# A two-layer hybrid mixer backbone on one core: reciprocals, TensorE's first waits, VectorE's share of the adaLN product, Fourier loads and the last square

## The chip, the cores and the metric

The kernel runs on one core of a Trainium2 chip. The metric is the time in microseconds (us) that the device reports for one execution; the median of several runs is given. The engines are TensorE (PE; its weight loads are listed as PEld), VectorE (DVE), ScalarE (ACT), GpSimd (POOL) and SyncE (SP). DMA transfers are issued here from the queues of SP and, where the text says so, of ACT; all of them share the core's 16 DMA engines.

## The reference

What is computed, cut to what matters:

```python
D_MODEL, SEQ, CTX_LEN, DEPTH = 2048, 256, 256, 2      # everything in float32

def rmsnorm(x, g):
    return x * lax.rsqrt(jnp.mean(x * x, axis=-1, keepdims=True) + EPS) * g

for l in range(DEPTH):
    last = l == DEPTH - 1
    shift, scale, gate = jnp.split(silu(c) @ ada_w[l] + ada_b[l], 3, axis=-1)
    shift_c, scale_c, gate_c = jnp.split(silu(c_ctx) @ ada_w[l] + ada_b[l], 3, axis=-1)
    h = rmsnorm(x, norm_g[l]) * (1.0 + scale[:, None]) + shift[:, None]
    hc = rmsnorm(xc, norm_g[l]) * (1.0 + scale_c) + shift_c
    # one projection to q, k, v, pool channels, Fourier channels and gate; k and v alone for hc in the last layer
    q, k, v, up, uf, g = split_proj(h @ w_in[l])
    ...
    att = latent_attention(rope(rmsnorm(q)), rope(rmsnorm(k)), v, kc, vc)
    mixed = concat([att, multiscale_pool(up, ...), fourier_mix(uf, fourier_w[l])])
    x = x + gate[:, None] * ((mixed * silu(g)) @ w_out[l])
    # in the first layer the same for xc, with attention to the context alone
return rmsnorm(x, final_norm_g)
```

The 256 latent and 256 context tokens stand side by side as 512 columns. The vectors c and c_ctx are the two "v" of the code.

## The kernel before

**Precision and weights.** A projection's matmul is done as three: each operand is split into a high part rounded for TensorE and a low rest. `wpiece` loads a piece of a weight matrix (raw), ACT casts it (whi) and DVE subtracts (wlo); the pool wp has three buffers of each, so the load of the fourth piece waits until DVE is done with the first. `make_h` makes the normed and modulated activations h of one 128-row block in the same two parts: DVE multiplies x by the reciprocal root (xn), scales and shifts it with the adaLN columns ab, ACT casts, DVE subtracts.

**The start (`startup`).** `stats(g)` squares four 128-row blocks of x (three squares on ACT, one on DVE), adds them in pairs on DVE, and PE multiplies each sum by a matrix of ones. That sums over partitions, for the latent half into the PSUM tile sm and for the context half into mm. `norm()` runs the last statistics, takes the roots of both halves on ACT and the reciprocal of the first; the second reciprocal stands in the loop, ahead of the second half of the first block's h.

The adaLN columns of shift and scale come in ten groups (`GROUPS`, of one or two 128-column blocks each). A group has four quarters of the 2048 input rows. `ND[j]` of them go to DVE: `dvec(j)` loads the quarter, and each scalar_tensor_tensor multiplies it by silu(c), which lies broadcast over the partitions in cq, and sums it into abq. The other quarters go to PE (`piece` loads one, `ada_part` issues four groups of 32-column matmuls with silu(c), cs, into one PSUM tile a). Then ACT copies a out (ev), PE transposes it, and DVE reduces it (red), adds the DVE quarters, the bias and the 1, and makes h. The silu(c) row that cq is broadcast from is made in `load_cb` from an input cb, stored to DRAM (cd) and read back by partition_broadcast.

There is one PSUM buffer of this kind, so the first `ada_part` of the next group waits until DVE's reduction has read the last. Between the pieces, `work(n)` issues up to n matmuls of a backlog: the products of the first input-projection chunk and of some gate columns with the h blocks that exist already. The order on PE in the start is exactly the written one (tc.manual_schedule); on the other engines a scheduler sorts by priority, which tc.high_priority changes (`DLOW`, -60, for the DVE quarters). Every DMA of the start is issued from SP's queue, and a load waits there until its buffer is free, with everything behind it; the ada quarters share four buffers (`ST`).

**After the start.** `pool_tables(0)` and `rope_tables(0)` load the tables of layer 0; `fourier_tables` loads its own (fw, the Fourier map; cct, the cosine matrices; dft) when the projection's second chunk runs, and PE forms cct times fw with them (L404). DVE meanwhile multiplies the next layer's adaLN weights (L189, ajunk<-araw,cbt). `pool_branch` has its last matmul in L347, and DVE evacuates it in L349.

**The end (`out_tok`).** The last output projection runs in four chunks of 512 columns with tokens on the partitions, two token tiles tt. `evac(a, ch, tt)` multiplies by the gate row (L758), adds the residual (L759) and squares with a running sum (L761). After chunk 3 it sums the four columns (L766), takes root and reciprocal (L767, L768), scales the four quarters on ACT and DVE (L773 to L777) and issues four stores (L778) for each tt.

Of the kernel before, what the change touches and what calls it, by code (L numbers as in the profile page):

```python
# [20 lines left out]
P = 128  # L21
# [12 lines left out]
ND = (0, 0, 0, 0, 0, 1, 1, 1, 2, 2)  # L34
# [14 lines left out]
LOW = -400  # L49
PRE = 6  # L50
# [5 lines left out]
def backbone(  # L56
# [4 lines left out]
    cb: bass.AP,  # L61
# [92 lines left out]
    def load_cb():  # L154
        crow = t2("crow", (32, P))
        nc.sync.dma_start(crow, cb)
# [217 lines left out]

    def pool_tables(l):
# [14 lines left out]
    def fourier_tables(l):  # L390
        fwt = t2("fw", (P, 512))
        nc.sync.dma_start(fwt, fw[l])
        cct = t2("cct", (P, 2, P))
        nc.sync.dma_start(cct, cc)
# [321 lines left out]
    def out_tok(xs, m, korder):  # L716
# [26 lines left out]
        side.add("turn", turn(), 2.0)  # L743
        ss = [sp.tile([P, 4], F32, tag=f"ssq{tt}", bufs=1, name=f"ssq{tt}") for tt in range(2)]
# [8 lines left out]
        def evac(a, ch, tt):  # L753
# [7 lines left out]
            S.activation(sq, x, AF.Square, accum_out=ss[tt][:, ch : ch + 1])  # L761
# [4 lines left out]
            V.tensor_reduce(r[:, 0:1], ss[tt], axis=AX.X, op=ALU.add)  # L766
            S.activation(r[:, 1:2], r[:, 0:1], AF.Sqrt, bias=epst, scale=1.0 / D)  # L767
            V.reciprocal(r[:, 1:2], r[:, 1:2])  # L768
            for q in (0, 3, 1, 2):
# [8 lines left out]
                nc.sync.dma_start(out[tt, :, cq_], o)  # L778
# [43 lines left out]
    load_cb()  # L822
# [6 lines left out]
    def startup():  # L829
        st = tc.tile_pool(name="st", bufs=ST)  # L830
        with st as st:
# [4 lines left out]
            S.activation(ctmp, cv, AF.Tanh, scale=0.5)  # L836
            V.tensor_scalar(ctmp, ctmp, 1.0, 0.5, op0=ALU.add, op1=ALU.mult)
            V.tensor_mul(cs[:, :, 0:2], ctmp.rearrange("p (k v) -> p k v", v=2), cv.rearrange("p (k v) -> p k v", v=2))
            rstd = const.tile([P, T], F32, tag="rstd", name="rstd0")
            dum = sp.tile([P, 1], F32, tag="dum", name="dum0")  # L840
            S.activation(dum, ctmp[:, 0:1], AF.Sqrt)
            ss = [smt(), mmt()]

            def stats(g):
                q = [t2("sq") for _ in range(4)]
                for j in range(4):
# [3 lines left out]
                    else:  # L850
                        S.activation(q[j], x, AF.Square)
                    if j % 2:
                        V.tensor_add(q[j - 1], q[j - 1], q[j])
                        for o, c in zip(ss, halves):
                            PE.matmul(o[:, :N], ones, q[j - 1][:, c], start=g == 0 and j == 1, stop=g == 3 and j == 3)
# [3 lines left out]
            def norm():  # L859
# [3 lines left out]
                V.reciprocal(rstd[:, halves[0]], rstd[:, halves[0]])  # L863
# [103 lines left out]

            with tc.manual_schedule(engines={mybir.EngineType.PE}):
                for g in range(3):
                    stats(g)  # L970
                for j, gs in enumerate(GROUPS):
# [4 lines left out]
                    for kk in range(npc):  # L976
                        if j == 0 and kk == 1:
                            load_x(3, 1)
                        if kk == npc - 1 and j + 1 < len(GROUPS):
# [9 lines left out]
                        ada_part(a, raws[kk], kk, kk == 0, kk == npc - 1, w_)  # L989
                        work(RATE * gs // 2)  # L990
                    ev = t2("ev")
                    S.copy(ev[:, :w_], a[:, :w_])
                    work(4)
                    for q in range(2 * gs):
                        PE.transpose(a[:, q * P : q * P + P], ev[:, q * P : q * P + P], idt)
                    work(4)
                    red = sp.tile([P, 2, gs, 2], F32, tag="red", name=name("red"))
                    V.tensor_reduce(
# [153 lines left out]
```

## Time and profile before

| | |
|---|---|
| median of 3 runs | 1078.14 us (1077.66 to 1080.66) |
| profiled execution | 1079.1 us, of which the profile's span is 1077.2 us |
| mean granted clock of TensorE | 0.992 |
| busy: PE / PEld / DVE / ACT | 97% / 78% / 79% / 45% of the span |
| moved by DMA | 234.15 MB, mean 217 GB/s |
| costliest lines on PE | L336, L337, L338 (the three matmuls of a product), 17% of the chain of waits each |

A row of the timeline gives the start and the duration in us, the engine, the line of the code, the operation, what it writes and reads, and the shape. In brackets stands the time for which the engine was idle just before, and what ended the wait. "SPq" rows are the issues of DMAs on SP's queue, where neighbours of one line are drawn together (x3). A row of the busy time by stretches gives the window, its length, the busy time of each engine with its count of instructions, and then the clock that TensorE was granted (1.00 is full), the busy share of the DMA engines and their GB/s. Times count from the span's start.

### The profile page before, as it was taken

How to read it: one execution, taken by the hardware profiler on the slowest of the kernel's cores; microseconds unless marked ns; L12 is line 12 of the kernel's file. 1: busy time of each engine (PE TensorE's matmuls, PEld its weight loads, DVE VectorE, ACT ScalarE, POOL GpSimd, SP SyncE). 2: the span in 40 equal slices, each digit the busy share in tenths (PEclk: the TensorE clock that was granted, in tenths of full speed). 3: DMA queues.
4: the chain of work that ended last, by engine and by line, in shares of the span. 5: the costliest groups of instructions: out<-in, count | busy, mean ns of one | idle time of the engine just before them, and what ended most of it. 6: DMA issues, size and time to landing. Idle time of an engine off the chain costs nothing.

```text
span 1077.2 us, 14001 instructions
## 1 busy us (share of the span) xinstructions
PE 1045.6 (97%) x5065; PEld 842.2 (78%) x5065; DVE 846.3 (79%) x1566; ACT 480.5 (45%) x807; POOL 0.2 (0%) x4
## 2 busy tenths in 40 slices
PE   5999899999999999999999999999999999999996
PEld 3466577788787888888888888888888888888885
DVE  6458656998999879997999887589656888776564
ACT  5233234323413765642532223288326768547443
POOL 0000000000000000000000000000000000000000
PEclk9999999999999999999999999999999999999998
DMA  9999857457685334457786657435765565776563
GB/s 355 414 368 345 277 200 239 157 190 233 200 266 195 96 122 155 157 195 259 251 286 218 198 195 262 139 127 190 246 229 170 159 195 184 236 262 215 180 213 115
DMA packets 64133, 234.15 MB, mean 217 GB/s; under 512 B 7153, under 2 KB 8257, under 8 KB 60353
## 3 DMA queue, kind: packets, MB, share of 16 engines
q1 hardware_dynamic: 64064, 233.28, 63.4%
q8 instruction: 39, 0.64, 0.3%
q14 instruction: 30, 0.24, 0.1%
HBM read 231.12 MB, written 2.12 MB: 217 GB/s over the span
## 4 chain that ended last, share of the span: by engine, by line
PE 66%; DVE 6%; issue 3%; ACT 1%; DMA 1%; ACTq 0%; SPq 0%; DVEq 0%
PE mm L336 17%; PE mm L338 17%; PE mm L337 17%; PE mm L312 5%; DVE ajunk L189 3%; PE mm L313 2%; PE sm L337 2%; PE sm L336 2%; PE sm L338 2%; DVE wlo L139 1%; PE sm L557 1%; DMA cbt<-cd 1%; PE sm L520 1%; DMA araw<-in_adar 0%; ACT whi L138 0%
## 5 line engine op out<-in xcount | busy, mean ns | idle before, releaser
L138 ACT CAST whi<-raw 128x1024 fp32r<-128x1024 f32 (+1 forms) x216 | 219.9, 1019 | 333.5 <-PE mm L338 108.5
L139 DVE TENSOR_TENSOR wlo<-raw,whi 128x1024 fp32r<-128x1024 f32 (+1 forms) x216 | 255.1, 1182 | 104.4 <-ACT whi L138 103.2
L189 DVE SCALAR_TENSOR_TENSOR ajunk<-araw,cbt 128x1024 bf16<-128x1024 f32 x224 | 273.6, 1221 | 48.5 <-DMA araw<-in_adar 35.2
L336 PE MATMUL mm<-whi,h 128*128 128x512 f32 x416 | 167.5, 403 | 0.0
L337 PE MATMUL mm<-wlo,h 128*128 128x512 f32 x416 | 162.8, 391 | 0.0
L338 PE MATMUL mm<-whi,h 128*128 128x512 f32 x416 | 162.8, 391 | 0.0
L336 PE MATMUL mm<-m,whi 128*128 128x512 f32 (+1 forms) x272 | 102.7, 377 | 0.0
L338 PE MATMUL mm<-m,wlo 128*128 128x512 f32 (+1 forms) x272 | 102.5, 377 | 0.0
L337 PE MATMUL mm<-m,whi 128*128 128x512 f32 (+1 forms) x272 | 102.5, 377 | 0.0
L312 PE MATMUL mm<-h,whi 128*128 128x512 f32 x256 | 92.5, 401 | 0.0
L338 PEld LDWEIGHTS mm<-whi,h 128*128 128x128 f32 x416 | 78.1, 188 | 16.9 <-DVE h L139 0.3
L337 PEld LDWEIGHTS mm<-wlo,h 128*128 128x128 f32 x416 | 78.3, 188 | 15.6 <-issue 1.4
L336 PEld LDWEIGHTS mm<-whi,h 128*128 128x128 f32 x416 | 78.3, 188 | 15.7 <-issue 1.4
L336 PE MATMUL mm<-h,whi 128*128 128x512 f32 x196 | 77.8, 397 | 0.2 <-DVE vl L139 0.2
L338 PE MATMUL mm<-h,wlo 128*128 128x512 f32 x196 | 76.8, 392 | 0.0
L337 PE MATMUL mm<-h,whi 128*128 128x512 f32 x196 | 76.7, 391 | 0.0
L313 PE MATMUL mm<-h,wlo 128*128 128x256 f32 x256 | 72.4, 283 | 0.0
L915 PE MATMUL mm<-whi,h 128*128 128x512 f32 x192 | 65.8, 413 | 1.9 <-ACT h L138 1.9
L337 PEld LDWEIGHTS mm<-m,whi 128*128 128x128 f32 x272 | 51.2, 188 | 9.5
L338 PEld LDWEIGHTS mm<-m,wlo 128*128 128x128 f32 x272 | 51.2, 188 | 9.4
L336 PEld LDWEIGHTS mm<-m,whi 128*128 128x128 f32 x272 | 51.2, 188 | 9.3
L312 PEld LDWEIGHTS mm<-h,whi 128*128 128x128 f32 x256 | 48.2, 188 | 10.8
(224 smaller groups left out, 1641.1 us busy)
## 6 DMA issues: line engine op xcount, KB each, us to landing
araw<-in_adar SPq DMA_DIRECT2D x128, 512.0 KB, 4.0
raw<-in_wb SPq DMA_DIRECT2D x78, 512.0 KB, 3.8
raw<-in_wg SPq DMA_DIRECT2D x55, 512.0 KB, 4.1
a<-in_ada SPq DMA_DIRECT2D x24, 1024.0 KB, 7.7
raw<-in_wo SPq DMA_DIRECT2D x32, 512.0 KB, 4.4
raw<-in_wot SPq DMA_DIRECT2D x32, 512.0 KB, 3.5
a<-in_ada SPq DMA_DIRECT2D x16, 512.0 KB, 5.4
x<-in_xT SPq DMA_DIRECT2D x4, 1024.0 KB, 7.5
```

The lines of the kernel that those rows point to most:

```text
L138: i = S.copy(hi, src)
L139: V.tensor_sub(lo, src, hi.bitcast(F32))
L189: V.scalar_tensor_tensor(junk, raw, 1.0, cbt[:, v], op0=ALU.mult, op1=ALU.mult, accum_out=acc[:, u, h, v : v + 1])
L312: PE.matmul(a.rearrange("p (s n) -> p s n", s=2), hi[:, j - j0], h.both[k][:, :, :N], start=s0, stop=False)
L313: PE.matmul(a[:, :N], lo[:, j - j0], h.hi[k][:, :N], start=False, stop=s1)
L336: PE.matmul(o, ah, bh, start=start, stop=False)
L337: PE.matmul(o, ah, bl, start=False, stop=False)
L338: PE.matmul(o, al, bh, start=False, stop=stop)
L520: PE.transpose(tp[:, hh * P : hh * P + P], qo[:, hh], idt)
L557: PE.transpose(tp[:, h * P : h * P + P], ps[h][:, i * P : i * P + P], idt)
L915: PE.matmul(o, lt, r, start=s0, stop=s1)
```

## The change

Six edits.

1. `load_cb` and its input are gone. Instead DVE copies silu(c) from cs (cvk), PE transposes it behind group 0's own transposes, ACT copies it to a row (`store_cb`), and SP stores it to DRAM ahead of the last piece of group 1.
2. `norm()` holds both reciprocals. In `stats(3)` PE sums both pairs of the latent half first and then both of the context half; before, the halves alternated. The dummy root that loads ACT's table is tied ahead of the first square. Group 0's part after the pieces gets a priority of its own (`CHAIN`).
3. `warm(n)` issues n matmuls of the matrix of ones by itself into a PSUM tile that is not yet in use: three before group 0's transposes, two behind, three and one behind the first two pieces of group 1: nine.
4. `ND` is 1 in the last two groups, not 2. A quarter of each goes from DVE to PE.
5. `fourier_loads` issues fw and cct for layer 0 with the pool tables.
6. In `out_tok` the square of chunk 3 is a scalar_tensor_tensor on DVE; the sum of the first three, divided by D and with EPS added, is made in chunk 2 and is the bias of the root; the stores of quarters 0 and 1 are issued from ACT's queue.

```diff
-ND = (0, 0, 0, 0, 0, 1, 1, 1, 2, 2)
+ND = (0, 0, 0, 0, 0, 1, 1, 1, 1, 1)
+CHAIN = 200
...
-    def load_cb():
+    def store_cb(cvk, tp):
+        PE.transpose(tp, cvk, idt)
         crow = t2("crow", (32, P))
-        nc.sync.dma_start(crow, cb)
-        ctmp2 = t2("ctmp2", (32, P))
-        silu(crow, crow, ctmp2)
+        S.copy(crow, tp)
...
-        nc.sync.dma_start(cd, crow)
+        late["store"] = lambda: nc.sync.dma_start(cd, crow)
...
+    def fourier_loads(l):
+        fwt = t2("fw", (P, 512))
+        nc.sync.dma_start(fwt, fw[l])
+        cct = t2("cct", (P, 2, P))
+        nc.sync.dma_start(cct, cc)
+        tabs.update(fw=(fwt, cct))
...
     def fourier_tables(l):
-        fwt = t2("fw", (P, 512))
-        nc.sync.dma_start(fwt, fw[l])
-        cct = t2("cct", (P, 2, P))
-        nc.sync.dma_start(cct, cc)
+        if l == 1:
+            fourier_loads(l)
+        fwt, cct = tabs["fw"]
...
-            S.activation(sq, x, AF.Square, accum_out=ss[tt][:, ch : ch + 1])
             if ch < 3:
+                S.activation(sq, x, AF.Square, accum_out=ss[tt][:, ch : ch + 1])
                 V.tensor_mul(x, x, f)
+                if ch == 2:
+                    r = rt[tt]
+                    V.tensor_reduce(r[:, 0:1], ss[tt][:, :3], axis=AX.X, op=ALU.add)
+                    V.tensor_scalar(r[:, 0:1], r[:, 0:1], 1.0 / D, EPS, op0=ALU.mult, op1=ALU.add)
                 return
-            r = sp.tile([P, 2], F32, tag="rt", name=name("rt"))
-            V.tensor_reduce(r[:, 0:1], ss[tt], axis=AX.X, op=ALU.add)
-            S.activation(r[:, 1:2], r[:, 0:1], AF.Sqrt, bias=epst, scale=1.0 / D)
+            r = rt[tt]
+            V.scalar_tensor_tensor(sq, x, 1.0, x, op0=ALU.mult, op1=ALU.mult, accum_out=ss[tt][:, 3:4])
+            S.activation(r[:, 1:2], ss[tt][:, 3:4], AF.Sqrt, bias=r[:, 0:1], scale=1.0 / D)
...
-                nc.sync.dma_start(out[tt, :, cq_], o)
+                (nc.sync if q > 1 else nc.scalar).dma_start(out[tt, :, cq_], o)
...
-                        for o, c in zip(ss, halves):
-                            PE.matmul(o[:, :N], ones, q[j - 1][:, c], start=g == 0 and j == 1, stop=g == 3 and j == 3)
+                pairs = [(o, c, j) for o, c in zip(ss, halves) for j in (0, 2)]
+                for o, c, j in pairs if g == 3 else sorted(pairs, key=lambda e: e[2]):
+                    PE.matmul(o[:, :N], ones, q[j][:, c], start=g == 0 and j == 0, stop=g == 3 and j == 2)
...
-                V.reciprocal(rstd[:, halves[0]], rstd[:, halves[0]])
+                for c in halves:
+                    V.reciprocal(rstd[:, c], rstd[:, c])
...
+            def warm(n):
+                for _ in range(n):
+                    PE.matmul(first[3][:, :P], ones, ones, start=True, stop=True)
...
+                        if j == 1 and kk == 3:
+                            late["store"]()
...
+                        if j == 1 and kk < 2:
+                            warm(3 - 2 * kk)
                         work(RATE * gs // 2)
...
                 pool_tables(0)
+                fourier_loads(0)
                 work(10 ** 6)
```

What becomes of the order on VectorE at the first h (group 0), before:

```order
L863 RECIPROCAL rstd_144<-rstd_144 128x256
L1012 RECIPROCAL rstd_144<-rstd_144 128x256
L139 TENSOR_TENSOR wlo_253<-raw_250,whi_252 128x512
L139 TENSOR_TENSOR wlo_259<-raw_256,whi_258 128x384
L998 TENSOR_REDUCE red_266<-sm_202 128x4
L249 TENSOR_TENSOR xn_270<-x_0_85,rstd_144 128x256
L1006 TENSOR_TENSOR ab_96<-red_266,vt 128x2x2
L249 TENSOR_TENSOR x_0_85<-x_0_85,rstd_144 128x256
L1007 TENSOR_TENSOR ab_96<-ab_96,vt 128x2
L256 TENSOR_SCALAR xn_270<-xn_270,ab_96 128x256
```

And at the same place after:

```order
L880 RECIPROCAL rstd_137<-rstd_137 128x256 x2
L1031 TENSOR_REDUCE red_270<-sm_193 128x4
L248 TENSOR_TENSOR xn_274<-x_0_85,rstd_137 128x256
L1039 TENSOR_TENSOR ab_96<-red_270,vt 128x2x2
L248 TENSOR_TENSOR x_0_85<-x_0_85,rstd_137 128x256
L1040 TENSOR_TENSOR ab_96<-ab_96,vt 128x2
L139 TENSOR_TENSOR wlo_245<-raw_242,whi_244 128x512
L255 TENSOR_SCALAR xn_274<-xn_274,ab_96 128x256
L255 TENSOR_SCALAR x_0_85<-x_0_85,ab_96 128x256
L139 TENSOR_TENSOR wlo_251<-raw_248,whi_250 128x384
```

The reciprocals stand in a row in both; the two wlo subtractions moved from ahead of the reduction (red) to behind it, one of them behind the scalings (L255).

VectorE where group 7 is finished, before. The rows of L948 are the DVE quarters (a_187 of group 8, a_200 and a_203 of group 9), wlo is a weight piece, red the reduction of group 7:

```order
L948 SCALAR_TENSOR_TENSOR a_187_1005,abq<-a_187_1005,cq_118 128x512 x2
L249 TENSOR_TENSOR xn_1058<-x_3_88,rstd_144 128x512
L249 TENSOR_TENSOR xn_1064<-x_3_88,rstd_144 128x512
L948 SCALAR_TENSOR_TENSOR junk_1086,abq<-a_200_1084,cq_117 128x512
L948 SCALAR_TENSOR_TENSOR junk_1089,abq<-a_200_1084,cq_117 128x512
L948 SCALAR_TENSOR_TENSOR a_200_1084,abq<-a_200_1084,cq_117 128x512
L948 SCALAR_TENSOR_TENSOR junk_1094,abq<-a_203_1092,cq_118 128x512
L948 SCALAR_TENSOR_TENSOR a_200_1084,abq<-a_200_1084,cq_117 128x512
L139 TENSOR_TENSOR wlo_1041<-raw_1038,whi_1040 128x1024
L998 TENSOR_REDUCE red_1053<-sm_942 128x8
```

And after, where L965 are the DVE quarters, a_183 of group 8 and a_197 of group 9:

```order
L965 SCALAR_TENSOR_TENSOR a_183_1003,abq<-a_183_1003,cq_106 128x512
L248 TENSOR_TENSOR xn_1056<-x_3_88,rstd_137 128x512
L248 TENSOR_TENSOR xn_1062<-x_3_88,rstd_137 128x512
L1031 TENSOR_REDUCE red_1051<-sm_950 128x8
L139 TENSOR_TENSOR wlo_1039<-raw_1036,whi_1038 128x1024
L1038 TENSOR_TENSOR red_1051<-red_1051,abq 128x8
L965 SCALAR_TENSOR_TENSOR junk_1097,abq<-a_197_1095,cq_106 128x512
L1039 TENSOR_TENSOR ab_96<-red_1051,vt 128x2x4
L965 SCALAR_TENSOR_TENSOR junk_1100,abq<-a_197_1095,cq_106 128x512
```

The reduction moved from behind five quarters' products and a wlo to directly behind the two xn.

SP's queue at the layer tables, before: the Fourier loads stand behind the weight pieces of chunk 1 (raw) and the first loads of the next layer's adaLN (araw).

```order
L145 DMA raw_1649<-in_wb 128x1024
L183 DMA araw_1395<-in_adar 128x1024
L145 DMA raw_1707<-in_wb 128x1024
L392 DMA fw_1459<-in_fw 128x512
L394 DMA cct_1461<-in_cc 128x256
L183 DMA araw_1401<-in_adar 128x1024
```

After, they stand behind the pool's bands and ahead of the rope tables:

```order
L389 DMA band_1287<-in_band 128x512
L376 DMA fw_1290<-in_fw 128x512
L378 DMA cct_1292<-in_cc 128x256
L453 DMA gqk_1370<-in_gqk 128x512
L145 DMA raw_1296<-in_wb 128x512
L455 DMA rope_1372<-in_rope 128x512
```

They moved ahead of thirteen other loads of SP's queue.

More of the change, by code (lines that the diff above doesn't have):

```diff
@@ L743, in out_tok @@
         side.add("turn", turn(), 2.0)
+        rt = [sp.tile([P, 2], F32, tag=f"rt{tt}", bufs=1, name=f"rt{tt}") for tt in range(2)]
         ss = [sp.tile([P, 4], F32, tag=f"ssq{tt}", bufs=1, name=f"ssq{tt}") for tt in range(2)]
@@ L1006, in startup @@
-                    V.tensor_add(dst, red, bias.unsqueeze(3).to_broadcast([P, 2, gs, 2]))
-                    V.tensor_mul(dst[:, 1], dst[:, 1], ng[:, k0 : k0 + gs].unsqueeze(2).to_broadcast([P, gs, 2]))
-                    for i in range(gs):
-                        k = k0 + i
-                        for vs in ((0,), (1,)) if k == 0 else ((0, 1),):
-                            if k == 0 and vs == (1,):
-                                V.reciprocal(rstd[:, halves[1]], rstd[:, halves[1]])
-                            make_h(h0, k, xk[k // 4][:, k % 4], rstd, 0, vs)
+                    with tc.high_priority(offset=CHAIN if j == 0 else 0):
+                        ev = t2("ev")
+                        S.copy(ev[:, :w_], a[:, :w_])
+                        if j:
+                            work(4)
+                        else:
+                            warm(3)
+                        for q in range(2 * gs):
+                            PE.transpose(a[:, q * P : q * P + P], ev[:, q * P : q * P + P], idt)
+                        if j:
+                            work(4)
+                        else:
+                            store_cb(cvk, a[:32, 2 * P : 3 * P])
+                            warm(2)
+                        red = sp.tile([P, 2, gs, 2], F32, tag="red", name=name("red"))
+                        V.tensor_reduce(
+                            red.rearrange("p w k v -> p (w k) v"), a[:, :w_].rearrange("p (q g r) -> p q r g", g=4, r=32)[:, :, 0:2, :],
+                            axis=AX.X, op=ALU.add,
+                        )
+                        dst = ab[0][:, :, k0 : k0 + gs]
+                        bias = adab[:, : 2 * KT].rearrange("p (w k) -> p w k", w=2)[:, :, k0 : k0 + gs]
+                        for e in range(ND[j]):
+                            V.tensor_add(red, red, abq[:, e, :, k0 : k0 + gs])
+                        V.tensor_add(dst, red, bias.unsqueeze(3).to_broadcast([P, 2, gs, 2]))
+                        V.tensor_mul(dst[:, 1], dst[:, 1], ng[:, k0 : k0 + gs].unsqueeze(2).to_broadcast([P, gs, 2]))
+                        for i in range(gs):
+                            k = k0 + i
+                            for vs in ((0,), (1,)) if k == 0 else ((0, 1),):
+                                make_h(h0, k, xk[k // 4][:, k % 4], rstd, 0, vs)
@@ L1099, in _layout @@
     )
-    t["cb"] = cv.reshape(32, P)
     ps, k0 = [], 0
```

31 lines of the change are left out of this document (10 added, 21 removed).

## The prediction

> **What bounds the kernel now.** I read the page first, then the busy time by stretches, then the timeline of the three places where TensorE (PE) stands still. The page's engine line and its chain of waits:
>
> ```profile
> PE 1045.6 (97%) x5065; PEld 842.2 (78%) x5065; DVE 846.3 (79%) x1566; ACT 480.5 (45%) x807; POOL 0.2 (0%) x4
> PE 66%; DVE 6%; issue 3%; ACT 1%; DMA 1%; ACTq 0%; SPq 0%; DVEq 0%
> ```
>
> PE is busy 1045.6 of 1077.2 us. The most that better waiting can give is therefore 31.6 us. The stretches show where those lie (the clock that PE was granted, the DMA share and GB/s are the last three columns):
>
> ```profile
> core 0: us, PE busy (x) PEld busy (x) DVE busy (x) ACT busy (x) POOL busy (x), PEclk, DMA share, GB/s
> 12.00:26.00 14.00, 9.54 (x75) 5.55 (x74) 9.87 (x18) 5.20 (x11) 0.00 (x0) 1.00 1.01 391
> 26.00:29.40 3.40, 3.40 (x11) 2.27 (x15) 1.36 (x3) 0.72 (x2) 0.00 (x0) 0.50 0.98 392
> 29.40:62.00 32.60, 30.80 (x173) 17.65 (x166) 13.29 (x26) 9.99 (x15) 0.00 (x0) 1.00 1.01 418
> 129.20:133.60 4.40, 0.02 (x2) 0.01 (x2) 2.62 (x7) 0.00 (x0) 0.00 (x0) 0.80 0.83 294
> 133.60:142.00 8.40, 8.40 (x38) 5.21 (x39) 5.48 (x17) 1.75 (x4) 0.00 (x0) 0.70 0.60 228
> 180.00:186.00 6.00, 4.44 (x18) 2.93 (x16) 5.96 (x8) 1.06 (x1) 0.00 (x0) 1.00 1.00 348
> 247.00:346.00 99.00, 97.43 (x434) 79.38 (x433) 93.25 (x174) 32.57 (x55) 0.00 (x0) 1.00 0.68 221
> ```
>
> Four things matter here. Up to 62 us the DMA engines are full (share 1.01), so there the data stream paces PE. Around 129 us PE stands still for a whole stretch and then works at a reduced clock, with DMA at 0.83: neither data nor PE paces it. At 180 us PE loses 1.56 us. From 180 to 346 us VectorE (DVE) is nearly always busy, so a gain of PE there counts only if DVE gains too.
>
> **The start: reciprocals, half order, warm matmuls, the silu row.** The load of the silu row on SP, and the rows from the root to the first matmul of the projection (brackets: the idle time before, and what ended it):
>
> ```profile
> 1.17 0.42 SPq L156 DMA_DIRECT2D crow<-in_cb  x1
> ...
> 19.22 0.47 ACT L862 ACTIVATE rstd<-sm,epst 128x256 f32<-128x256 f32 x1 [3.37 <-PE sm L855]
> 19.65 0.47 ACT L862 ACTIVATE rstd<-mm,epst 128x256 f32<-128x256 f32 x1
> 19.72 1.75 DVE L863 RECIPROCAL rstd<-rstd 128x256 f32<-128x256 f32 x1 [2.42 <-ACT rstd L862]
> 21.11 0.44 PE L995 MATMUL sm<-idt,ev 128*128 128x128 f32 x2 [0.49 <-ACT ev L992]
> 21.39 1.69 DVE L1012 RECIPROCAL rstd<-rstd 128x256 f32<-128x256 f32 x1
> 22.16 0.64 PE L964 MATMUL sm<-a,cs 128*32 128x256 f32 x8 [0.62 <-DMA a<-in_ada]
> 23.00 1.09 DVE L139 TENSOR_TENSOR wlo<-raw,whi 128x512 fp32r<-128x512 f32 x2
> 23.39 0.64 PE L964 MATMUL sm<-a,cs 128*32 128x256 f32 x8 [0.59 <-DMA a<-in_ada]
> 25.93 0.77 PE L915 MATMUL mm<-whi,h 128*128 128x512 f32 x1 [1.90 <-ACT h L138]
> ```
>
> The two reciprocals already follow one another on DVE (19.72 and 21.39); writing them together moves neither. What moves is what stands behind them. Both wlo subtractions (1.09 together, from 23.00) now stand behind the first reduction, one ahead of the two scalings and one behind, which brings the first h forward by about 0.5. Summing half 0 of the statistics to its end before half 1 lets the first root start one 128x256 matmul earlier: the two roots are 0.43 apart. The load of the silu row and its store no longer stand among the x loads on SP, and DVE and ACT lose its silu; that brings the squares forward by that issue, 0.42 (the row at 1.17). Sum: 0.5 + 0.43 + 0.42, about 1.4, so the first L915 matmul falls at about 24.5 instead of 25.93.
>
> The row now comes out of a PE transpose, an ACT copy and a store that stands on SP behind the weight load that waits for a wlo. It is read from group 5 on; it delays only the ada loads queued behind it on SP, by one issue of about 0.4.
>
> Nine matmuls of 128x128 are added in PE's waits. The transposes at 21.11 have that size: 0.22 each, 2.0 for nine. They fit in the waits of 0.49, 0.62, 0.59 and 1.90 (3.6 in all), so I cost them at nothing; without that cover they cost 2.0. What they could buy is the clock: 26.00 to 29.40 ran at 0.50, which is 1.7 of lost work. The window before it had PE busy only a part of the time, though no single wait in it was over 1.90.
>
> The Trainium skill ("TensorE: Matmul & The Clock Gate", section "HAM oscillation — how this bites in real kernels") gives as its abstract rule that PE idle gaps over about 3.4 us cost the clock. By it the drop at 26 us would have needed a longer wait than any here, the warm matmuls would buy nothing, and the start's advance would be 1.4 instead of 3.1, and the rival "the start's advance lasts whole" would come to 1069.7. The trace disagrees with it (1.90 was enough).
>
> So PE would be 1.4 + 1.7 = 3.1 ahead at 29 us. How much lasts? From 29.40 to 62 us PE idles 1.80 of 32.60 while the DMA share is 1.01: PE takes its ada pieces as they land, and the stream's bytes are the same. Bounds: nothing lasts (the stream decides, and a queue slot of 0.4 more or less changes sides), or all 3.1 lasts. I take 0.4, near the lower end, since the share of 1.01 is nearer to "the stream decides".
>
> **The groups 8 and 9: one quarter on VectorE instead of two.** DVE's queue and PE's around the stop:
>
> ```profile
> 128.03 0.69 DVE L948 SCALAR_TENSOR_TENSOR a<-a,cq 128x512 f32<-128x512 f32 x1
> 130.98 0.69 DVE L948 SCALAR_TENSOR_TENSOR junk<-a,cq 128x512 f32<-128x512 f32 x1 [2.26 <-DMA a<-in_ada]
> 133.35 0.18 DVE L998 TENSOR_REDUCE red<-sm 128x8 f32<-128x32 f32 x1
> 133.59 1.08 PE L964 MATMUL sm<-a,cs 128*32 128x256 f32 x8 [4.38 <-DVE red L998]
> 137.89 0.98 PE L964 MATMUL sm<-a,cs 128*32 128x256 f32 x8
> 142.66 0.64 PE L964 MATMUL sm<-a,cs 128*32 128x256 f32 x8
> 143.79 0.63 PE L915 MATMUL sm<-h,whi 128*128 128x512 f32 x2
> 144.26 0.39 PE L915 MATMUL sm<-h,wlo 128*128 128x512 f32 x1
> 145.05 0.64 PE L964 MATMUL sm<-a,cs 128*32 128x256 f32 x8
> ```
>
> The reduction of group 7 stands behind a quarter's product that waits 2.26 for its data, a second product and a wlo. PE has one PSUM tile for these sums, so the first ada matmul of group 8 waits 4.38 for that reduction. In the new order the reduction stands directly behind two xn products, ahead of every product of group 9; the late data then delay only the products, which nobody on PE waits for before group 9's own sum. So 4.38 goes. What is late next is h of group 7, behind three products: PE has backlog matmuls of other columns to do meanwhile, as between 133.59 and 145.05.
>
> The stop also cost clock. From ada piece to ada piece with seven matmuls between took 4.30 (133.59 to 137.89) against 2.39 (142.66 to 145.05), a loss of 1.91; the next piece took 0.98 against 0.64, a loss of 0.34. Together 2.25, which goes with the stop.
>
> Eight products of 0.69 leave DVE (5.5, off PE's path) and with them the second broadcast of the silu row, two DMAs of 256 KB. Two pieces of 128x256 come to PE. Seven matmuls at 0.235 (143.79 to 144.26 is two) are 1.6 of the 2.39 between two pieces; a piece costs the remaining 0.8, two 1.6. They run on the path, since PE is busy there. Net: 4.38 + 2.25 - 1.6 = 5.0. Bounds: 2.8 if the clock still drops (a shorter stop left over), 5.4 if a piece costs only its busy 0.64.
>
> **The Fourier tables, loaded with the pool's.**
>
> ```profile
> 178.23 0.42 SPq L394 DMA_DIRECT2D cct<-in_cc  x1
> 184.44 1.96 PE L404 MATMUL sm<-fw,cct 128*128 128x512 f32 x4 [1.56 <-DMA cct<-in_cc]
> 190.12 0.88 DVE L349 SCALAR_TENSOR_TENSOR mix<-sm,vt,icnt 128x256 f32<-128x256 f32 x2 [1.47 <-PE sm L347]
> ```
>
> Issued at 178.23, the table releases PE at 184.44 after 1.56 of waiting. Issued some 25 us earlier, before the rope tables, it is there. The two issues (0.42 each) move ahead on SP into a stretch with the DMA well under full (0.60 from 133.60 on), so they cost nothing there; without that cover they delay the loads behind them by 0.85. PE gains 1.56, but DVE is the fuller engine from here to 346 us. Its own wait of 1.47 for PE (190.12) is the only one of that kind, and it shortens with PE's. Bounds 0 and 1.6; I take 1.5, because these two rows are of one size.
>
> **The tail.**
>
> ```profile
> 1067.78 6.14 SPq L778 DMA_DIRECT2D out<-res  x8
> 1069.18 0.69 DVE L759 TENSOR_TENSOR res<-res,og 128x512 f32<-128x512 f32 x1
> 1069.90 0.63 ACT L761 ACTIVATE sq<-res 128x512 f32<-128x512 f32 x1 [1.54 <-DVE res L759]
> 1070.44 0.19 ACT L761 ACTIVATION_READ_ACCUMULATOR sq<-res 128x1 f32 x1
> 1070.66 0.16 DVE L766 TENSOR_REDUCE rt<-ssq 128x1 f32<-128x4 f32 x1 [0.79 <-ACT sq L761]
> 1070.85 0.29 ACT L767 ACTIVATE rt<-rt,epst 128x1 f32<-128x1 f32 x1 [0.22 <-DVE rt L766]
> 1071.37 1.33 ACT L777 ACTIVATE res<-res,rt 128x512 f32<-128x512 f32 x2 [0.23 <-DVE rt L768]
> ```
>
> The last square moves to DVE, right behind the add: 0.69 like the products above, instead of 0.63 and 0.19 with a change of engine. The sum of the other three goes ahead. From the add's end (1069.87) that gives, with 0.1 for the change to ACT, a root at 1070.70 instead of 1070.85: 0.15. The two small DVE operations added in chunk 2 (about 0.3 to 0.6) lie beside PE's work of that chunk. All eight stores stood on SP until 1073.92, though the last scaled quarter is ready at 1072.70; with half of them on ACT's queue the last is issued some 0.35 sooner. Together 0.5, between 0 (the last landing decides alone) and 1.0.
>
> **The sum.** 0.4 + 5.0 + 1.5 + 0.5 = 7.4 us. The profiled execution took 1079.1 (span 1077.2 and 1.9 around it), 0.96 above the median of 1078.14 and inside the runs' 1077.66 to 1080.66, so I apply the sum to the median: 1070.7.
>
> **Rivals.**
> - The start's advance lasts whole. For it: only 1.80 of PE idle up to 62 us, so PE has work of other columns. Against it: the full DMA. It adds 2.7: 1068.0.
> - The stop at 129 us is replaced in part. For it: group 8's and 9's pieces must now land for PE itself (DMA 0.83, one piece landed at 130.98), and the clock then drops again. Against it: PE's order puts seven matmuls between two pieces. 2.26, that wait, moves to PE, and 2.25 of clock comes back: 7.4 - 4.5 = 2.9 left, 1075.2.
> - DVE absorbs what PE gains before 346 us: the Fourier gain is nothing and 1 of group 8's as well: 1073.2. For it: DVE's 5.96 of 6.00 and 93.25 of 99; against it: PE loses only 1.57 of those 99, so it is PE that is mostly followed.
> - Slower: the store of the row blocks SP. It waits for a PE transpose and an ACT copy; every ada load to 62 us is queued behind it, and the stream is full, so each us that it comes late is a us of PE lost, plus 1.7 for each clock window. It decides when the store is issued over some 5 us late, past 30 us: 5 + 3.4 + the 2.0 of warm matmuls that lost their cover, against 7.0 of gains elsewhere: 1081.5. Against it: the transpose follows at 22 us directly on the two at 21.11, and the load before it on SP waits to about 23.6 anyway.
> - The rearrangement does nothing that can be measured: the stop's wait is only renamed, and the rest gives 2.4: 1075.7.
>
> **How the numbers follow.** No change that a measurement of this kernel can tell is within 0.3%, 3.2 us. Forecast 0.60; start whole 0.10; DVE absorbs 0.12; stop replaced 0.07; nothing measurable 0.06; slower 0.04; the missing 0.01 goes to the middle. Faster by over 3.2 us is forecast, start whole and DVE (0.82) and some of the cases at 1075, 0.05: 0.87; same 0.09; slower 0.04. The range: from 1067.5 (start whole, with the tail at its 1.0) to 1074.6 (group 8 at its lower bound of 2.8, Fourier 0, start 0.4, which is 1074.4). The forecast alone holds 1069 to 1072.5.
>
> **What would show it.** Right: PE's wait for red of group 7 under 0.5 and the clock at 1.00 from 29 to 1070 us; L409 (the table's matmul, before L404) without a wait for cct; the first L932 matmul at 24.5 and no half clock at 26 us; ada pieces between 30 and 60 us landing at the old times; the last store issued before 1066.5. Wrong: a clock of 0.5 anywhere after 30 us, PE waiting for a<-in_ada by over 4 us in all up to 62 us, or DVE's idle time between 180 and 346 us grown by what PE won.

## The result, and the profile after

| | before | after |
|---|---|---|
| median | 1078.51 us (6 runs, 1077.66 to 1080.66) | 1072.26 us (6 runs, 1071.91 to 1073.19) |
| ratio | | 0.994, 95% interval 0.9928 to 0.9951 |
| span of the profiled execution | 1077.2 us | 1071.4 us |
| mean granted clock | 0.992 | 0.998 |

The kernel is 6.25 us faster, where 7.4 was forecast. The profiled execution of the new kernel took 1073.19, the slowest of its six. The same stretches as before the change, with the one ahead of 26 us:

```profile
22.60:26.00 3.40, 3.17 (x21) 1.96 (x22) 3.15 (x11) 1.35 (x3) 0.00 (x0) 1.00 0.77 263
26.00:29.40 3.40, 3.15 (x19) 1.68 (x17) 0.65 (x2) 0.51 (x1) 0.00 (x0) 1.00 0.81 273
29.40:62.00 32.60, 29.14 (x160) 16.68 (x160) 13.86 (x27) 9.46 (x14) 0.00 (x0) 1.00 1.02 419
129.20:133.60 4.40, 4.40 (x30) 2.69 (x30) 4.40 (x16) 1.25 (x2) 0.00 (x0) 1.00 0.77 267
133.60:142.00 8.40, 8.40 (x54) 5.54 (x47) 5.21 (x12) 2.88 (x4) 0.00 (x0) 1.00 0.72 250
180.00:186.00 6.00, 6.00 (x34) 4.91 (x33) 5.97 (x12) 2.90 (x5) 0.00 (x0) 1.00 0.82 234
247.00:346.00 99.00, 97.57 (x438) 79.53 (x437) 97.59 (x185) 34.77 (x58) 0.00 (x0) 1.00 0.68 216
```

The stop at 129 us and both stretches at half clock are gone. From 22.6 to 29.4 us the DMA engines are no longer full (shares 0.77 and 0.81), which was not forecast. The rows of the start from the first root to the first projection matmul (L932):

```profile
18.54 0.47 ACT L878 ACTIVATE rstd<-sm,epst 128x256 f32<-128x256 f32 x1 [3.02 <-PE sm L871]
19.04 3.37 DVE L880 RECIPROCAL rstd<-rstd 128x256 f32<-128x256 f32 x2 [2.05 <-ACT rstd L878]
23.16 0.68 DVE L139 TENSOR_TENSOR wlo<-raw,whi 128x512 fp32r<-128x512 f32 x1
23.91 0.33 SPq L145 DMA_DIRECT2D raw<-in_wgs  x1
24.34 0.38 SPq L160 DMA_DIRECT2D cd<-crow  x1
24.66 0.50 PE L932 MATMUL mm<-whi,h 128*128 128x512 f32 x1 [0.23 <-ACT h L138]
24.77 2.27 SPq L976 DMA_DIRECT2D a<-in_ada  x3
```

The end, from the last projection matmul's evacuation on (og is its first operation, the product with the gate row):

```profile
1060.60 6.35 SPq L788 DMA_DIRECT2D out<-res  x4
1062.64 0.69 DVE L764 TENSOR_TENSOR og<-mm,grow 128x512 f32<-128x512 f32 x1 [1.68 <-PE mm L337]
1064.09 0.69 DVE L776 SCALAR_TENSOR_TENSOR sq<-res 128x512 f32<-128x512 f32 x1
1064.83 0.29 ACT L777 ACTIVATE rt<-ssq,rt 128x1 f32<-128x1 f32 x1 [3.67 <-DVE sq L776]
1066.10 0.95 ACTq L788 DMA_DIRECT2D out<-res  x2
```

From og (1062.64) to the end of the span it takes 8.76; before, from og (1068.45), 8.72. The tail by itself has gained nothing. Of the signs that the prediction named, one failed here: the last store was issued at 1066.72, not before 1066.5.

Effects of a few tenths of a us are smaller than the spread of runs (about 1 us either way), so the experiments below are also read by landmarks: how much earlier (negative) the same TensorE matmuls start than in the trace of before, as the median over all matmuls that stand in both programs, in a stretch of before's time. The last column is the start of the last og. Where two traces of the same code differ, that is the spread to keep in mind.

```
                    60-70  125-130  150-160  190-200  300-330  480-600  1020-1040  last og
after               -0.66    -0.62    -5.70    -6.53    -6.64    -6.11      -6.38    -5.81
after, 2nd trace    -0.95    -0.92    -6.01    -6.77    -6.09    -5.55      -6.66    -6.23
e1_nd_alone          0.79     0.78    -4.24    -5.02    -4.65    -4.56      -4.80    -4.79
e2_red_first         0.76     0.76    -3.68    -4.46    -4.18    -4.12      -4.04    -4.04
e3_warm8             0.97     0.97    -1.67    -1.88    -2.07    -1.97      -2.56    -2.56
e4_no_warm           1.55     1.59    -3.49    -5.18    -4.63    -4.09      -4.62    -4.19
e5_fourier_late     -0.58    -0.53    -5.61    -6.40    -6.23    -5.59      -5.85    -5.42
e6_stores_sp        -0.51    -0.48    -5.56    -7.22    -7.08    -6.61      -6.68    -6.26
e7_less_stream      -2.65    -2.61    -7.69    -9.22    -9.67    -7.97      -8.37    -7.95
e8_order_and_nd2    -0.38    -0.34    -4.82    -6.52    -7.01    -6.44      -5.58    -5.16
e9_warm_early       -0.64    -0.61    -5.69    -7.39    -7.19    -6.62      -6.99    -6.57
e10_raw_own         -1.50    -1.46    -6.54    -8.24    -8.27    -7.71      -7.92    -7.29
e12_aligned         -1.56    -1.56    -6.58    -7.76    -7.87    -7.90      -8.35    -8.10
```

The kernel's own gains stand in the first row: 0.62 in the start, 5.08 at groups 8 and 9, 0.83 at the Fourier tables, 0.57 lost in the last chunk (0.43 in the second trace). e1, e2 and e3 have the start of before unchanged and still lie 0.76 to 0.97 later at 65 us than the one trace of before; the section on the start comes back to that.

### The profile page after: what moved, and what is told of

It is laid out like the page before. It is cut to its first block, busy times and chain, and to the rows that moved or that the text cites. A ratio compares the mean times of both kernels' runs of the same rounds, so it can differ in the third digit from the quotient of the medians.

```text
span 1071.4 us, 14049 instructions
## 1 busy us (share of the span) xinstructions
PE 1047.4 (98%) x5100; PEld 842.6 (79%) x5100; DVE 842.3 (79%) x1553; ACT 479.7 (45%) x803; POOL 0.2 (0%) x4
## 4 chain that ended last, share of the span: by engine, by line
PE 81%; DVE 7%; DMA 4%; ACT 3%; issue 3%; SPq 0%; DVEq 0%; ACTq 0%
PE mm L336 18%; PE mm L335 18%; PE mm L337 18%; PE mm L932 6%; PE mm L311 5%; PE sm L932 3%; DVE ajunk L188 2%; DMA a<-in_ada 2%; PE mm L312 2%; PE sm L336 2%; PE sm L337 2%; PE sm L335 2%; PE sm L981 2%; DVE wlo L139 2%; PE sm L562 1%
## 5 line engine op out<-in xcount | busy, mean ns | idle before, releaser
L932 PE MATMUL mm<-whi,h 128*128 128x512 f32 x192 | 63.8, 401 | 0.2 <-ACT h L138 0.2
```

Source lines behind the costliest of these rows:

```text
L932: PE.matmul(o, lt, r, start=s0, stop=s1)
```

## The experiments

### Groups 8 and 9: amount of work, order, or clock

For this place the landmarks in finer steps. From the first column to the second the wait for group 7's reduction shows, from the second to the third the clock behind it, from the third to the last what is given back.

```
                  125-130   133-134   139-141   150-160
after               -0.62     -5.06     -7.30     -5.70
e1_nd_alone          0.78     -3.68     -5.92     -4.24
e2_red_first         0.76     -3.70     -5.88     -3.68
e3_warm8             0.97      0.54     -1.68     -1.67
e8_order_and_nd2    -0.34     -4.78     -7.02     -4.82
```

**e1_nd_alone.** Edit, in the kernel before:

```diff
-ND = (0, 0, 0, 0, 0, 1, 1, 1, 2, 2)
+ND = (0, 0, 0, 0, 0, 1, 1, 1, 1, 1)
```

> The kernel before with one quarter of groups 8 and 9 on VectorE instead of two, nothing else. Theory: the stop at 129 us (4.38) and its half clock (2.25) go, two pieces of 0.8 come to TensorE: 5.0 us faster, and from 150 us on every landmark lies 5.0 to 5.1 earlier. Rival (the gain at that place needs the earlier start too, or comes from the lighter SP queue of the other edits): 3 us or less.

1073.93 us against 1077.86, ratio 0.9963 (0.9952 to 0.9974): 3.9 faster, with an interval of 2.8 to 5.2 that just holds the 5.0. The landmarks go from 0.78 to -4.24: 5.02, which is the theory's figure; their level is 0.8 off the theory's -5.0, because the start lies that much later in this trace. One thing more: at the Fourier tables another 0.78 comes, without any edit to them. (A row of waits gives who waited for what, the us in total, how often, and the longest.)

```profile
PE sm L404 <- DMA cct<-in_cc: 0.8, 1, 0.8
```

The wait for cct (1.56 before) has halved by itself.

**e2_red_first.** Edit, in the kernel before: a dependence that moves no data keeps each product of group 9 behind group 7's reduction.

```diff
-                                V.scalar_tensor_tensor(
+                                i = V.scalar_tensor_tensor(
 ...
+                                if j == 9:
+                                    tc.add_manual_dep(i.ins, late["red"].ins.name, ...)
```

> The kernel before, still with two quarters of groups 8 and 9 on VectorE; only the order of VectorE's queue is changed: group 9's products may not stand ahead of group 7's reduction. Theory (it is the order, not the amount of work on VectorE): the stop and its clock go and no piece comes to TensorE: 6.0 to 6.6 us faster. Rival (VectorE has too much to do there; the late products then delay the sums of groups 8 and 9): 0 to 2 us faster, with a new wait of TensorE for a reduction between 133 and 145 us.

1074.18 us, ratio 0.9964 (0.9953 to 0.9975): 3.7 faster. Up to 140 us the landmarks gain 6.64 (0.76 to -5.88): the order alone removes stop and half clock.

```profile
129.20:133.60 4.40, 4.40 (x30) 2.45 (x29) 4.40 (x15) 0.40 (x2) 0.00 (x0) 1.00 1.02 370
133.60:142.00 8.40, 6.51 (x40) 3.85 (x38) 7.94 (x23) 2.53 (x5) 0.00 (x0) 1.00 0.72 245
```

Then 2.2 are given back, 1.9 of them in two new waits (PE's waits from 120 to 150 us):

```profile
PE sm L1000 <- ACT ev L997: 1.2, 1, 1.2
PE sm L969 <- DVE red L1003: 0.7, 1, 0.7
```

So both sides are partly right. The order made the stop. With the second quarter on VectorE come these waits, and 2.2 are lost where the two pieces on PE cost 1.6 (changed kernel) and 1.7 (e1). Whether VectorE's products or the missing pieces on TensorE make the waits was not separated: the longer one is for a copy that ACT makes behind a weight cast.

**e3_warm8.** Edit, in the kernel before, ahead of group 8's first piece (z is a tile of zeros):

```diff
+                        if j == 8 and kk == 0:
+                            for _ in range(18):
+                                PE.matmul(accs[0][:, :P], z, ones, start=False, stop=False)
```

> The kernel before with 18 extra 128x128 matmuls of zeros on TensorE (added to an open sum, so they change nothing) inside its stop at 129 us. The wait for the reduction stays. Theory (the clock is a term of its own, 2.25): the granted clock stays 1.00 from 129 to 142 us and the kernel is 2.0 to 2.3 us faster. Rival (matmuls behind the stop are paced by VectorE or by data, not by the clock): under 0.5 us faster. Rival 2 (the clock follows waits over about 3.4 us; the extra matmuls fill the wait): as the theory.

1076.17 us, ratio 0.9982 (0.9973 to 0.9992): 1.7 faster; by landmarks 2.64. Of these, 0.43 is there at the first matmul behind the stop, which came that much sooner in this trace, and 2.2 follow by 140 us. The wait is filled, and the clock stays:

```profile
129.20:133.60 4.40, 4.40 (x38) 4.23 (x37) 3.32 (x9) 0.30 (x1) 0.00 (x0) 1.00 0.95 370
133.60:142.00 8.40, 8.40 (x56) 5.42 (x55) 6.78 (x23) 2.35 (x4) 0.00 (x0) 1.00 0.67 226
```

The clock was a term of its own, 2.2 against the 2.25 that the prediction took.

**e8_order_and_nd2.** The changed kernel with the old ND and the dependence of e2.

> The changed kernel with two quarters of groups 8 and 9 on VectorE again, and group 9's products kept behind group 7's reduction. Theory (order alone removes the stop): the two pieces of 0.8 leave TensorE and no stop comes back: 1.6 us faster than the changed kernel, about 1070.7. Rival (two quarters on VectorE are too late): 1 to 5 us slower than the changed kernel.

1072.71 us (ratio to before 0.9952, 0.9934 to 0.997), the same as the changed kernel. At groups 8 and 9 it gains 4.48 instead of 5.08, because it gives back 2.2 behind the stop, as e2 does. Neither theory nor rival came true.

### The start: clock, stream or instruction fetch

**e4_no_warm.** `warm(n)` issues nothing.

```diff
             def warm(n):
-                for _ in range(n):
+                for _ in range(0):
```

> The changed kernel without the nine extra matmuls of ones. Theory (up to 62 us the data stream paces TensorE, the clock matters little there): the half clock of 26 to 29.4 us comes back, TensorE is 1.3 to 1.7 us later at 30 us, but at 65 us at most 0.3 later than in the changed kernel; time the same within 0.3 us. Rival (the start's advance lasts): 1.3 to 1.7 us slower than the changed kernel.

1073.21 us (ratio to before 0.9953, 0.9935 to 0.9971); too close to tell by time. By landmarks the theory missed: 2.2 later at 65 us than the changed kernel's first trace (2.5 against its second, 2.1 against e6), and 1.8 of it was still there at 1030 us. The clock fell as expected:

```profile
22.60:26.00 3.40, 1.77 (x11) 0.91 (x12) 3.23 (x12) 1.46 (x4) 0.00 (x0) 0.87 0.72 240
26.00:29.40 3.40, 3.40 (x16) 1.78 (x16) 0.69 (x1) 0.05 (x1) 0.00 (x0) 0.63 0.99 290
```

But the trace shows another difference. A load has 16 parts, one for each DMA engine, and is done with the last. For the first piece of group 2 the first part, the last part, and the start of the 16 KB instruction fetch nearest to it were:

```
                 first part   last part   instruction fetch
before                29.63       32.21   30.2
after                 31.32       31.86   24.6
e4_no_warm            31.17       34.05   30.0
e9_warm_early         31.26       31.87   24.6
e10_raw_own           28.90       31.05   24.6
```

In e4 the load's first part comes as early as in the changed kernel, the last 2.2 later. The profile lists the fetch as a queue kind of its own; for e4 from 29 to 31 us (packets, MB, share):

```profile
q8 instruction: 1, 0.02, 2.9%
```

**e9_warm_early.** The nine matmuls ahead of the first statistics instead.

```diff
             with tc.manual_schedule(engines={mybir.EngineType.PE}):
+                warm(9)
                 for g in range(3):
                     stats(g)
```

> The changed kernel with its nine extra matmuls of ones ahead of the first statistics instead of around groups 0 and 1, where they can't hold the clock at 26 us. Background: without the nine (e4_no_warm) TensorE was 2.1 us later at 65 us, and in that trace one of the 16 DMA engines lagged 1.5 to 2 us behind the others from a 16 KB instruction fetch at 30.0 us on; with the nine the fetch came at 24.6 us, while the DMA engines were not full. Theory (what lasts of the nine is that they move the fetch, by their count): half clock again at 26 us, but the fetch at 24 to 26 us, the last DMA engine less than 0.8 behind, and landmarks at 65 us within 0.5 of the changed kernel. Rival (what lasts is the clock, or the time of the work itself): about 2 us later at 65 us, as without the nine.

1072.42 us (ratio to before 0.9949, 0.9933 to 0.9966). The clock falls, and the landmarks at 65 us are those of the changed kernel (-0.64):

```profile
22.60:26.00 3.40, 1.80 (x11) 1.09 (x12) 3.21 (x11) 1.49 (x4) 0.00 (x0) 0.74 0.77 271
26.00:29.40 3.40, 3.40 (x18) 2.09 (x17) 0.69 (x1) 0.01 (x1) 0.00 (x0) 0.75 0.74 278
29.40:62.00 32.60, 30.07 (x165) 17.09 (x163) 13.90 (x27) 9.99 (x15) 0.00 (x0) 1.00 1.02 418
```

In this kernel the half clock at 26 us costs nothing that lasts: TensorE is 0.92 later than the changed kernel at 30 us and 0.02 at 34. What lasts of the nine is that there are nine more instructions: the fetch comes at 24.6 us, while the DMA engines have gaps (share 0.77), and not at 30 us into a full stream, where one engine then lags behind. Two things speak for that beyond these runs. In all fourteen traces this fetch starts when 199 to 210 of TensorE's matmul and weight-load records have begun. And the changed kernel shows it a second time: its next such fetch, at 50.3 us, meets a full stream, and within two loads the last part falls from 0.54 to 2.06 behind the first.

With before's start, a longer loss of clock did last. In e1, e2 and e3 the half clock went from 24.2 to 24.6 us until 31.0 to 31.4, in before's own trace from 25.99 to 29.40. From 18 to 30 us these traces are within 0.2 of before's, from 30 us on they are 0.74 to 0.94 later, and stay so to 65 us.

**e7_less_stream.** The gate weights' two parts are split from an x tile and not loaded, so the gate columns that the start computes are other numbers.

```diff
-                e = pick(wgs[w], NE * P, k0, n)
+                split(xk[3][:, :n, : NE * P], e_hi, e_lo)
```

> The changed kernel without the loads of the gate weights of the start: their two parts are made from an x tile that is there already, so the gate columns come out of other numbers, and 1.9 MB less flow up to 62 us (4.6 us at 418 GB/s). Theory (the stream paces TensorE there): TensorE's waits for the adaLN data between 26 and 62 us (2.6 in the changed kernel) nearly vanish, and landmarks at 65 us lie 2 to 3 us earlier than in the changed kernel. Rival (VectorE's chain or TensorE's own order paces the start): under 0.5 us earlier.

1070.89 us (ratio to before 0.9938, 0.9922 to 0.9953). Landmarks at 65 us: -2.65, 2.0 earlier than in the changed kernel. From 24 to 62 us TensorE has no wait over 0.71, where the changed kernel had 0.90 and 1.17. The stream does pace the start.

```profile
22.60:26.00 3.40, 3.17 (x21) 1.95 (x22) 3.17 (x11) 1.35 (x3) 0.00 (x0) 1.00 1.04 394
26.00:29.40 3.40, 3.40 (x27) 1.84 (x25) 0.60 (x2) 0.51 (x1) 0.00 (x0) 1.00 1.01 414
```

**e10_raw_own.** The first two weight pieces take buffers of their own, so the fourth load doesn't wait for VectorE.

```diff
-            raw = wp.tile(list(shape), F32, tag="raw", name=name("raw"))
+            if late.get("st") and shape[1] == 1 and late["raws"]:
+                late["raws"] -= 1
+                raw = late["st"].tile(list(shape), F32, tag=f"raw{late['raws']}", bufs=1, name=name("raw"))
+            else:
+                raw = wp.tile(list(shape), F32, tag="raw", name=name("raw"))
```

> The changed kernel with buffers of their own for the first two weight pieces of the start, so that the load of the fourth piece on SP (at 23.9 us) no longer waits for VectorE's first wlo with the adaLN loads queued behind it. Theory (that wait empties the DMA engines: share 0.77 to 0.81 from 22.6 to 29.4 us, 1.4 us of stream, which is where the start's advance went): share 0.95 or more there, landings from 29 us on 1.4 earlier, landmarks at 65 us 1.0 to 1.4 earlier, time 1 us or more below the changed kernel. Rival (the instruction fetch at 24.6 us then meets full DMA engines and one of them lags): landings 0.3 to 0.6 earlier, time within 0.5 us.

1071.68 us, and 1072.40 for the changed kernel of the same call (ratios to before 0.9945 and 0.9949, intervals overlap). Landmarks at 65 us: -1.50 against -0.66 and -0.95, between theory and rival.

```profile
22.60:26.00 3.40, 3.40 (x23) 2.28 (x23) 3.14 (x10) 0.94 (x3) 0.00 (x0) 1.00 1.05 403
26.00:29.40 3.40, 3.40 (x26) 1.61 (x25) 1.11 (x2) 1.13 (x2) 0.00 (x0) 1.00 1.03 425
```

The gap in the stream was SP's wait, as the theory says: the load's first part is 2.4 earlier (28.90 against 31.32). The last part is only 0.8 earlier, because the fetch at 24.6 us now meets full DMA engines.

### Fourier loads, stores, and once more

**e5_fourier_late.**

```diff
-        if l == 1:
-            fourier_loads(l)
+        fourier_loads(l)
 ...
-                fourier_loads(0)
```

> The changed kernel with fw and cct loaded late again, as before the change. Theory (the wait for cct is half replaced by a wait for VectorE's th): TensorE waits again 1.5 for cct, landmarks behind 190 us lie 0.8 us later, time +0.8 us against the changed kernel. Rival (the prediction's 1.5): +1.5. Rival (VectorE is the bound there): 0.

1073.87 us (6 runs, 1073.20 to 1075.49; ratio to before 0.9966, 0.9954 to 0.9978), against 1072.49 (4 runs, 1071.84 to 1072.72) for e6, which has the early loads. The landmarks gain 0.79 between 160 and 190 us, as in e1; e6 gains 1.66, the changed kernel 0.83 and 0.76 in its two traces. So by the traces the edit is worth 0 to 0.9, and the first half of the prediction's 1.5 comes from the groups' edit. By the times it is worth more: 1.4 between the medians, and no run of the one kernel reaches those of the other. The profiled execution of e5 was one of its faster ones, that of e6 the slowest of its four, and the traces show only these. The rival's 1.5 is therefore not refuted.

**e6_stores_sp.**

```diff
-                (nc.sync if q > 1 else nc.scalar).dma_start(out[tt, :, cq_], o)
+                nc.sync.dma_start(out[tt, :, cq_], o)
```

> The changed kernel with all eight stores of the output on SP's queue. Theory (four stores of 256 KB land at the rate of the DMA engines, about 0.65 us each, whichever queue issues them): from the first issue to the last landing 4.2 us as with two queues, time the same within 0.2 us. Rival (issue time decides): 0.35 to 0.4 us slower.

1072.49 us (ratio to before 0.9949, 0.9933 to 0.9965). From the first issue of the last four stores to the last landing: 4.22 with one queue, 4.22 with two, 4.17 before. The issue takes 1.80 instead of 0.95:

```profile
1065.65 1.80 SPq L788 DMA_DIRECT2D out<-res  x4
```

Four stores of 256 KB land 0.6 to 0.7 apart from one queue and in pairs from two, and the last of them lands equally long behind the first issue; the queue doesn't matter. The Trainium skill ("DMA: Bandwidth & Descriptors", section "Issuing engines are not separate DMA queues") says that issuing from several engines saves only the sequencer's time to issue. The trace agrees: 0.85 of issue saved, 0.00 of landing.

**e11_again.** The changed kernel, unaltered.

> The changed kernel once more, to see what repeats. In its first trace TensorE waited 0.57 for VectorE's th in front of L409 and gained 0.8 at the Fourier tables; in e6_stores_sp, the same code up to the tail, there was no such wait and the gain was 1.66. Theory (that wait is chance, the edit is worth about 1.5 here): no wait over 0.2 and a gain of 1.5 to 1.7 between 172 and 190 us. Rival (it belongs to the changed kernel): 0.57 again. Its last matmuls, at a pitch of 0.233 instead of 0.227 in the first trace from 1039 us on: same in every trace if it belongs to the code.

1072.40 us (ratio to before 0.9949, 0.9933 to 0.9965). The wait is there again:

```profile
PE sm L409 <- DVE th L829: 0.7, 1, 0.7
```

(th is the gate columns' tanh, which VectorE finishes.) It is absent in e6 and e9, which don't touch that place, and in e4, e7, e8 and e10; there the gain is 1.53 to 1.70. e12 has 0.2 of it and gains 1.18. So it belongs to the changed kernel, but not always; which delay in the start decides it was not tried. The pitch (the distance between the starts of two matmuls) of 0.233 in the last chunk came again too.

**e12_aligned.** e10 with two buffers for each rt tile, which nothing uses.

```diff
-        rt = [sp.tile([P, 2], F32, tag=f"rt{tt}", bufs=1, name=f"rt{tt}") for tt in range(2)]
+        rt = [sp.tile([P, 2], F32, tag=f"rt{tt}", bufs=2, name=f"rt{tt}") for tt in range(2)]
```

> The kernel of e10_raw_own, with 64 bytes a partition more in the pool of small tiles (two buffers instead of one for each of the two rt tiles). Background: the changed kernel's rt tiles take 64 bytes less than before, so every pool laid out behind (the weight parts in f4 among them) starts at 64 beyond a multiple of 128 bytes; in the last chunk, of 96 matmuls, those that read a weight part from f4 have a pitch of 0.233 us instead of 0.227 in all four traces of the changed tail, and the chunk takes 22.57 to 22.77 us instead of 22.15. Theory (the address sets the pitch): all 96 at 0.227, the chunk at 22.15 us, and the kernel 0.4 to 0.6 us below e10_raw_own, about 1071. Rival (the squares and sums on VectorE beside the matmuls slow them): 0.231 on the mean as before, 22.6 us.

1070.70 us (6 runs, 1068.73 to 1070.94; ratio to before 0.9933, 0.9916 to 0.995), against 1071.68 for e10 and 1072.26 for the changed kernel: the fastest of all. In the last chunk, six matmuls apart, the changed kernel and then e12:

```profile
1058.96 0.39 PE L335 MATMUL mm<-whi,m 128*128 128x512 f32 x1
...
1060.36 0.39 PE L335 MATMUL mm<-whi,m 128*128 128x512 f32 x1
```

```profile
1056.75 0.39 PE L339 MATMUL mm<-whi,m 128*128 128x512 f32 x1
...
1058.11 0.39 PE L339 MATMUL mm<-whi,m 128*128 128x512 f32 x1
```

1.40 against 1.36, that is 0.2333 and 0.2267 for one. A row's duration (0.39) hides it; only the distance of the starts shows it. In e12 the pitch is 0.227 throughout, but for one stop of 0.24 in the chunk (e10 and the first trace of the changed kernel have it too) that makes it 22.39 long instead of the 22.15 expected. The changed kernel's chunk holds both kinds: by the addresses in the built programs, 48 of its 96 matmuls read a moving operand (the one that streams through the array, here the weight part) that starts 64 bytes beyond a multiple of 128, and their median pitch is 0.233; the others start at a multiple, and theirs is 0.227. In before and in e12 all 96 start at a multiple. The drift shows it over a longer stretch: from 300 to 600 us every trace with the shorter rt tiles loses 0.47 to 0.64 (e7 more, with a wait of 1.85 of its own there), and e12 nothing (-7.87 to -7.90); from 1040 us to the last og they lose 0.42 to 0.63, e12 0.25, its stop. That makes about 0.9 in all.

## Why the prediction was right, and where its terms were off

**The start** (0.4 forecast, 0.62 and 0.92 in two traces against before's own): the first matmul came at 24.66 (24.5 forecast), the clock held, and of the 3.1 forecast for 29 us the trace shows 2.2 to 2.5, which shrink to 0.64 by 48 us. The size fits against before's own trace alone: against e1, e2 and e3, which have the same start and lost more clock, the gain is 1.4 to 1.9, so that the 0.4 came out is in part luck. The reason was half right. The stream does decide (e7), but it was not simply full: the fourth weight load waits on SP for the first wlo, which is no earlier than before (issue at 23.91), with the ada loads behind it. That issue before the change:

```profile
23.66 0.33 SPq L145 DMA_DIRECT2D raw<-in_wgs  x1
```

As the x loads had moved up, the engines ran dry for some 20% of 6.8 us. I had named that wait and costed only the store's issue. And the warm matmuls, costed as a question of clock, act in this kernel by their count (e4, e9).

The Trainium skill ("TensorE: Matmul & The Clock Gate", section "HAM oscillation — how this bites in real kernels") ties the loss of clock to idle gaps above 3.4 us. The runs disagree: the clock fell at 25.10 us in e4 and at 24.26 in e9, and in the 3.41 us ahead of that no wait was over 1.2, with TensorE busy 1.51 and 1.83.

**Groups 8 and 9** (5.0 forecast, 5.08 measured; e1 alone 5.02): right, term by term. The landmarks of the changed kernel gain 4.44 at the stop (4.38 forecast) and 2.24 with the clock behind it (2.25 forecast; 2.2 in e3), and give back 1.60 for the two pieces (1.6 forecast). The stop was a matter of order, as argued, but with two quarters on VectorE 2.2 would have been lost even in a good order (e2), which I had not seen.

**The Fourier tables** (1.5 forecast, 0.83 and 0.76 in the changed kernel's two traces, 1.53 to 1.70 in the six traces without the wait for th; 1.4 between the medians of e5 and e6): the size is right in some executions and half of it in others. The step that fails in the latter is "it shortens with PE's": a wait of 0.57 to 0.65 for VectorE's th takes the place of the rest. And half of the old wait is gone without the edit (e1, e5), which the forecast did not foresee. The rival that VectorE absorbs the gain had this right for these executions, but not for group 8's gain, which passed whole.

**The tail** (0.5 forecast, -0.5 measured at the last og, nothing behind it): two steps failed. The last square on VectorE brought the first store 0.21 closer to og (3.46 against 3.67), as said, and the last landing 0.16 (7.68 against 7.84), but the span then ended 1.08 behind that landing instead of 0.88. The stores' issue time was no limit (e6). And "the sum of the other three goes ahead" hid a cost that no row of before could show: the two new rt tiles (the small tiles for sum and root) take 64 bytes less than the buffers of the old one, everything laid out behind them moved, and the matmuls that read weight parts there slowed by 3%.

The sum of what was forecast is 7.4; with the Fourier term at 0.8, the tail at -0.5 and the start at 0.6 it is 5.9, against 6.25 by the medians and 5.8 by the two profiled spans.

## What to carry to other kernels

When an engine's order puts a product that waits for data ahead of a small reduction that another engine waits for, move the reduction and not only the work, and count the clock that the stop costs as a term of its own. A gain on TensorE while the DMA queue is full lasts only as far as the loads come earlier: look at what the queue's next load waits for. Compare the distance between matmul starts, not only their durations, after any change of a tile's size, however small. A trace shows one execution: where it and the medians disagree, as in e5, a term read from it stays open.

## What the runs showed of the hardware that I had not expected

- A 16 KB instruction fetch on one DMA engine during a full stream leaves that load's last part 2 to 3 us behind its first (before, e4, e10), against 0.5 to 0.6 where the fetch fell into a gap (after, e9); in e7 and e12, with a full stream, it was 1.7 and 1.9. The number of TensorE instructions ahead decides when it comes: nine more matmuls moved it from 30.0 to 24.6 us.
- A moving operand of 128x512 fp32r that starts 64 bytes beyond a multiple of 128 gave a matmul pitch of 0.2333 us, at a multiple of 128 0.2267, in the changed kernel's last chunk side by side. The slow ones all read one pool's tiles, and in e12, where that pool starts at a multiple, it is fast, so the pool as such is not the cause. Other offsets than 64 were not tried.
- The granted clock fell behind stretches of 3.41 us in which TensorE was busy 0.82 and 0.92 us (before, 128.39 and 22.58 us), 1.51 (e4) and 1.83 (e9), and it held behind fuller ones, but also behind one with 1.82 in the changed kernel. So the busy time alone does not tell; what does, no run here shows. e9 ahead of the fall, then the changed kernel, which kept its clock:

```profile
20.85:24.26 3.41, 1.83 (x19) 0.58 (x19) 3.41 (x9) 1.42 (x4) 0.00 (x0) 1.00 1.03 401
43.30:46.71 3.41, 1.82 (x16) 0.68 (x20) 2.44 (x8) 1.18 (x3) 0.00 (x0) 1.00 1.02 418
```
